# Delayed attention units, weight products in traced order, later norm steps and a split last norm in a decoder layer

## The chip, the cores and the metric

The kernel runs on one core of one Trainium2 chip. The metric is the device time of one execution in microseconds (us). The core's engines are named as in the profile: PE (TensorE, matrix products; PEld is its weight load), DVE (VectorE), ACT (ScalarE), POOL (GpSimd) and SP (SyncE, which here only issues DMAs). Each engine works through its own list of instructions in order; semaphores tie the lists together.

## The reference

One decoder layer on 256 tokens of width 2048, in fp32. `D_FF` is 5632.

```python
def swiglu(h, w_gate, w_up, w_down):
    return (jax.nn.silu(h @ w_gate) * (h @ w_up)) @ w_down
...
    x = x + 0.5 * swiglu(rms_norm(x, ffn1_norm), ...)
    x = gated_parallel_mixer(x, mix_norm, w_in, ...)
    x = memory_cross_attention(x, mem, cross_norm, ...)
    x = x + 0.5 * swiglu(rms_norm(x, ffn2_norm), ...)
    return rms_norm(x, final_norm)
```

The mixer multiplies the normed x by `w_in` and sends parts of the result two ways. One is attention within a window of 128 tokens, with 16 heads in 4 groups and a sink added to each softmax:

```python
    m = jnp.maximum(jnp.max(s, axis=-1, keepdims=True), sink)
    e = jnp.exp(s - m)
    p = e / (jnp.sum(e, axis=-1, keepdims=True) + jnp.exp(sink - m))
```

The other is a recurrent token mixing (RWKV-7) with a state of 64 by 64 for each of 16 heads. For it the keys are shifted between neighbouring tokens, normalised (`kk / max(sqrt(sum(kk*kk)), 1e-12)`, the "removal keys") and weighted with a decay and a rate. Both results are projected, gated with a sigmoid, added and multiplied by `w_out`.

## The kernel before

**Products.** Every fp32 weight is loaded by SP into `raw` and split into two parts: `hi`, a rounding cast on ACT (L396), and `lo`, the residue on DVE (L397). The activations are split the same way (`xhi`, `xlo`). A product is then three matmuls, written by `times` in lines L473, L474 and L475, which add up in an accumulator `acc` in PSUM. There are three buffers of `acc`, three of `mm` and two of `tr`. `multiply` does `KU` = 2 slices of the inner dimension for one half of the tokens, so it issues six matmuls (a "group of six"). `product` loops over the weight units of a column block and over the two halves of the tokens, and calls `bg.tick()` after each group of six.

**Background steps.** `bg` is an `Interleave`: named groups of Python generators. A tick lets the first generators of each group (two in "attn" and "chain", four in "stage", one in the others) run on to their next `yield`. `idle(n)` yields n times, `wait_for(name)` yields until a name has been reported. So the distance between two steps is counted in ticks, that is, in groups of six. This fixes the order in which the instructions are traced. A scheduler behind it may move instructions of an engine against that order, where tiles and buffers allow; `tc.issue_after(ins)` keeps what is written under it behind the instruction `ins`.

**Attention.** `attend(kv, qb)` handles one group of heads and one block of 128 queries: scores (L903), scale and bias (L909), maximum (L916 to L923), exponentials with their sums on ACT (L926, L928), normalisation on DVE (L936), transposes (L942) copied to `pt` on ACT (L945), and the product with v (L950), split into `yahi` (L957) and `yalo` (L958). Eight such generators are spawned in the order kv, qb; two run at a time.

**Columns.** `columns` multiplies by `w_in`, scales the result into `tok` (L847, ACT), transposes it (L661) into `p` (L975, ACT), forms the difference of neighbours `d` (L978, POOL) and the mix of both (L982, DVE). `decay_and_rate` loads its small weights `wa` with two DMAs on POOL's queue (L1009, L1010) and multiplies by them (L1023). `removal_keys(h)` does the normalisation: sums of squares on PE (L1081), root on ACT (L1082), maximum and reciprocals on DVE (L1084, L1086), the factors of `kk` (L1088 to L1099), products `kk` by `at` (L1118) and their mask (`lt`, L1124). The blocks `lt` go to DRAM (`ld`) and come back by four SP loads as `dl` (L1139) for a triangular substitution on DVE (L1146). Gates (`ga`) take a sigmoid on ACT (L1168) and a product on DVE (L1171). The chain of the token mixing (L1249 transposes, L1255 `mk`, L1286 to L1329 products) runs beside later columns, and `stage` (L376 to L388) forms sums of weights for the second feed-forward from tiles `su` and `sg`.

**Output projection and norms.** The product with `w_out` is added to x on DVE (L1480). Then `n3.block` transposes x (L661), scales it into `xhi` (L688) and `xlo` (L689) and takes squares (L697). In the last feed-forward `done2` adds up squares of a finished block of 512 columns (L1587, ACT) and multiplies the block by the final gain (L1589, POOL). After the last matmul come the sum (L769), its squares, the mean (L707, L708), the power on POOL (L710), the scaling (L1601 to L1605) and the store (L1608).

Of the kernel before, what the change touches and what calls it, by code (L numbers as in the profile page):

```python
# [136 lines left out]
def decoder_layer(ctx: ExitStack, tc: tile.TileContext, a: dict, out: bass.AP):  # L137
# [31 lines left out]
    def wait_for(name):  # L169
        while name not in bg.seen:  # L170
            yield

    def idle(n):
        for _ in range(n):
            yield


    ones = cpool.tile([P, P], F32, name="ones")
    pool.memset(ones[:], 1.0)
# [148 lines left out]
    raws, parts, summed = {}, {}, {}  # L328
    first_unused = {items[i][0][1] for i in staged}
    sums_d = dram.tile([len(staged), P, 4, 512], F32, name="sums")  # L330
    at = {"item": 0, "product": 0, "pool": None}

    def load(u, pieces=None):

# [135 lines left out]
    def times(o, x, w, first, last, **how):  # L470

        (xh, xl), (hi, lo) = x, w
        pe.matmul(o, xh, hi, start=first, stop=False, **how)  # L473
        pe.matmul(o, xh, lo, start=False, stop=False, **how)  # L474
        pe.matmul(o, xl, hi, start=False, stop=last, **how)  # L475

    def multiply(o, x, u, k, t, nk):
        s = slice(t * P, (t + 1) * P)
        for i in range(KU):
            times(  # L480
                o, [x.at(p, k + i)[:, s] for p in range(2)], [w[:, i, :] for w in u],
                k + i == 0, k + i == nk - 1,
            )

    def combinations(sp, x: Act, seven, name, ready=lambda: True, early=True, n=0):

# [227 lines left out]
    def feed_forward(sp, x, norm: Norm, wg, wu, wd, done, begin_last=lambda: None, last=False):  # L714
# [13 lines left out]
        for gi, (j0, nj) in enumerate(GROUPS):  # L728
            h = Act(
                [sp.tile([P, 16, T], F32R, tag="hhi", name="hhi")],  # L730
                [sp.tile([P, 16, T], F32R, tag="hlo", name="hlo")], 16,
            )
            ch = combinations(sp, h, SEVEN_DOWN[nj < 4], "d", early=False, n=12)

            def transposed(hb, c):
                for q in range(2):
                    split(h, c + 2 * q, 2, feat(hb, [2 * q * P, (2 * q + 1) * P]))
                    yield

            for j in range(j0, j0 + nj):  # L740
                if j > 0:
                    hb = gate_and_up(sp, norm.x, c, norm.r, wg)

                    c["next"].append(transposed(hb, 4 * (j - j0)))
                    continue
                pg = product(norm.x, wg)
                hb = sp.tile([P, 2, 512], F32, tag="hb", name="hb", bufs=2)
                for t in range(2):
                    act.activation(hb[:, t, :], pg[t][:], AF.Silu, scale=norm.r[t])
                pu = product(norm.x, wu)  # L750
                for t in range(2):
# [12 lines left out]
            for n in (0, 2):  # L764
                if last and end and n:
                    for m in (n, n + 1):
                        pd = product(h, wd, skew=m == 3)
                        for t in range(2):
                            dve.scalar_tensor_tensor(  # L769
                                col(t, m), pd[t][:], 0.5, col(t, m), ALU.mult, ALU.add  # L770
                            )
                        done(m)
                    continue
                down(sp, h, ch, wd, [[col(t, n + i) for i in range(2)] for t in range(2)])
                if end:
                    done(n)
                    done(n + 1)
# [11 lines left out]

    def aligned(sp):  # L790

        sp.tile([P, 16], F32, name="shift")


    with tc.tile_pool(name="f1", bufs=1, reuse_waits="tile") as sp:
# [32 lines left out]
    with tc.tile_pool(name="mx", bufs=1, reuse_waits="tile") as sp:  # L828
# [645 lines left out]
        for n in range(4):  # L1474
# [3 lines left out]
            po = product(mt, W["w_out"])  # L1478
            for t in range(2):
                dve.tensor_tensor(s[:, t, :], po[t][:], s[:, t, :], ALU.add)  # L1480
            bg.spawn("feat", n3.block(n, s))
            if n == 0:
                bg.spawn("mem", memory())

# [70 lines left out]


    with tc.tile_pool(name="f2", bufs=1, reuse_waits="tile") as sp:
        aligned(sp)
        at["pool"] = sp
        x = sp.tile([P, 2, D], F32, name="x")  # L1560
        fins = []
# [1 line left out]
        def fin(n):  # L1563

            return fins[n // 2][:, n % 2]

        def gain():
            for n in range(4):
# [3 lines left out]
                pool.dma_start(fin(n), a["final_norm"][cb].unsqueeze(0).broadcast_to([P, 512]))  # L1572
                yield

        def reload():
            for n in range(4):
                cb = slice(n * 512, (n + 1) * 512)
# [1 line left out]
                pool.dma_start(x[:, :, cb], blk(x3d, n))  # L1579

        bg.spawn("const", reload())
        ss = stat.tile([P, 2, 4], F32, tag="ss", name="ss")

        def done2(n):
            for t in range(2):
                xs = x[:, t, n * 512 : (n + 1) * 512]
                act.activation(junk_t[:], xs, AF.Square, accum_out=ss[:, t, n : n + 1])  # L1587
# [51 lines left out]
```

## Time and profile before

| what | value |
|---|---|
| median of three runs | 2249.39 us (2248.35 to 2249.53) |
| profiled execution, own time | 2248.79 us |
| its span, first to last instruction | 2247.1 us |
| mean granted clock of TensorE | 0.999 |
| PE / PEld busy | 2231.4 / 1833.6 us |
| DVE / ACT / POOL busy | 1820.5 / 1245.0 / 134.9 us |
| mean DMA throughput | 205 GB/s |

A row of the timeline reads: start in us from the span's start, duration in us, engine, line, operation, output and inputs by tile name, shapes, number of instructions, and in brackets the idle time of the engine just before and what ended it. Several like instructions that follow each other are one row (x4), and its duration runs over all of them. In the view of waits a row reads: engine, tile and line that waited, engine, tile and line waited for, total us, number of times, longest. A matmul's duration in a row holds its passage through the array, so matmuls of 0.39 us start about 0.227 us apart.

### The profile page before, as it was taken

To read this page: it belongs to the slowest core of one execution; us is meant where nothing else is said; L and a number is where in the kernel's file an instruction comes from. 1 tells how busy PE (TensorE), PEld (TensorE's weight loads), DVE (VectorE), ACT (ScalarE), POOL (GpSimd) and SP (SyncE) were. 2 spreads that over 40 slices of the span, in tenths; PEclk is the share of its full clock that TensorE was granted. 3 is DMA by queue.
4 is the path that set the end of the run, shared out by engine and by line. 5 is a ranking of instruction groups with operands and counts; after the bars stand their busy time and mean duration, and the time that the engine had idled before them with its cause. 6 is when DMAs were issued, how large, how long until landed. Compare 5 with 4: busy or idle time off the path is not lost.

```text
span 2247.1 us, 28239 instructions
## 1 busy us (share of the span) xinstructions
PE 2231.4 (99%) x10587; PEld 1833.6 (82%) x10587; DVE 1820.5 (81%) x2342; ACT 1245.0 (55%) x1621; POOL 134.9 (6%) x192
## 2 busy tenths in 40 slices
PE   9999999999999999999999999999999999999998
PEld 7888888888888877788888888888888888888886
DVE  7898988998989476977656666547999999999997
ACT  6555555555556567544444446456665466555654
POOL 1000000000001000201320040001000000000002
PEclk9999999999999999999999999999999999999999
DMA  7555555556556544676767576547565566556564
GB/s 264 187 201 197 201 198 202 200 188 212 195 193 201 169 135 150 198 231 207 224 214 263 187 258 227 190 167 272 197 237 204 195 231 218 201 205 221 197 229 146
DMA packets 229225, 461.35 MB, mean 205 GB/s; under 512 B 15227, under 2 KB 17504, under 8 KB 229088
## 3 DMA queue, kind: packets, MB, share of 16 engines
q1 hardware_dynamic: 220512, 433.62, 56.8%
q0 software_dynamic: 8112, 25.12, 3.5%
q8 instruction: 83, 1.36, 0.2%
q10 hardware_dynamic: 464, 0.79, 0.1%
q14 instruction: 54, 0.44, 0.1%
HBM read 435.91 MB, written 23.59 MB: 204 GB/s over the span
## 4 chain that ended last, share of the span: by engine, by line
PE 95%; DVE 2%; DMA 1%; issue 1%; ACT 1%; SPq 0%; POOL 0%; POOLq 0%; DVEq 0%; ACTq 0%
PE acc L473 19%; PE acc L474 19%; PE acc L475 19%; PE mm L475 8%; PE mm L474 8%; PE mm L473 8%; PE tr L661 2%; PE tr L474 2%; PE tr L473 2%; PE tr L475 2%; PE mm L1313 1%; DVE lo L397 1%; PE tr L1249 1%; DMA raw<-in_w_out_dram 0%; PE mm L903 0%
## 5 line engine op out<-in xcount | busy, mean ns | idle before, releaser
L396 ACT CAST hi<-raw 128x1024 fp32r<-128x1024 f32 (+1 forms) x770 | 756.5, 992 | 714.4 <-PE acc L475 514.8
L397 DVE TENSOR_TENSOR lo<-raw,hi 128x1024 fp32r<-128x1024 f32 (+1 forms) x770 | 886.1, 1153 | 315.5 <-ACT hi L396 314.0
L473 PE MATMUL acc<-hi,xhi 128*128 128x512 f32 (+1 forms) x1166 | 462.2, 397 | 2.1 <-ACT xhi L688 1.7
L474 PE MATMUL acc<-lo,xhi 128*128 128x512 f32 (+1 forms) x1166 | 452.7, 388 | 0.0
L475 PE MATMUL acc<-hi,xlo 128*128 128x512 f32 (+1 forms) x1166 | 452.5, 388 | 0.0
L473 PEld LDWEIGHTS acc<-hi,xhi 128*128 128x128 f32 x1166 | 219.4, 188 | 49.8 <-issue 4.0
L475 PEld LDWEIGHTS acc<-hi,xlo 128*128 128x128 f32 x1166 | 218.8, 188 | 46.0 <-DVE xlo L689 1.0
L474 PEld LDWEIGHTS acc<-lo,xhi 128*128 128x128 f32 x1166 | 219.2, 188 | 43.8 <-issue 1.7
L404 ACT CAST thi<-raw 128x1024 fp32r<-128x1024 f32 x192 | 199.9, 1052 | 62.9 <-DVE raw L427 42.4
L405 DVE TENSOR_TENSOR tlo<-raw,thi 128x1024 fp32r<-128x1024 f32 x192 | 232.2, 1219 | 1.1 <-ACT thi L404 0.4
L474 PE MATMUL acc<-lo,hhi 128*128 128x512 f32 x372 | 145.5, 391 | 0.8 <-DVE lo L397 0.8
L475 PE MATMUL acc<-hi,hlo 128*128 128x512 f32 x372 | 145.5, 391 | 0.0
L473 PE MATMUL mm<-hi,xhi 128*128 128x512 f32 x370 | 145.4, 393 | 0.0
L473 PE MATMUL acc<-hi,hhi 128*128 128x512 f32 x372 | 144.9, 390 | 0.0
L475 PE MATMUL mm<-hi,xlo 128*128 128x512 f32 x370 | 144.3, 390 | 0.0
L474 PE MATMUL mm<-lo,xhi 128*128 128x512 f32 x370 | 144.2, 390 | 0.0
L474 PEld LDWEIGHTS acc<-lo,hhi 128*128 128x128 f32 x372 | 69.9, 188 | 15.4 <-DVE lo L397 1.2
L473 PEld LDWEIGHTS acc<-hi,hhi 128*128 128x128 f32 x372 | 69.9, 188 | 14.3
L475 PEld LDWEIGHTS mm<-hi,xlo 128*128 128x128 f32 x370 | 69.4, 188 | 14.6
L475 PEld LDWEIGHTS acc<-hi,hlo 128*128 128x128 f32 x372 | 69.9, 188 | 14.0
L474 PEld LDWEIGHTS mm<-lo,xhi 128*128 128x128 f32 x370 | 69.5, 188 | 14.2
L473 PEld LDWEIGHTS mm<-hi,xhi 128*128 128x128 f32 x370 | 69.5, 188 | 14.0
(396 smaller groups left out, 3595.7 us busy)
## 6 DMA issues: line engine op xcount, KB each, us to landing
raw<-in_ffn_w_down_dram SPq DMA_DIRECT2D x88, 1024.0 KB, 5.1
raw<-in_ffn_w_gate_dram SPq DMA_DIRECT2D x84, 1024.0 KB, 5.1
raw<-in_ffn_w_up_dram SPq DMA_DIRECT2D x78, 1024.0 KB, 6.2
raw<-in_w_in_dram SPq DMA_DIRECT2D x136, 512.0 KB, 3.5
raw<-in_w_out_dram SPq DMA_DIRECT2D x32, 512.0 KB, 4.4
raw<-sums SPq DMA_DIRECT2D x20, 512.0 KB, 6.3
raw<-in_w_proj_attn_dram SPq DMA_DIRECT2D x16, 512.0 KB, 4.4
raw<-in_w_proj_rwkv_dram SPq DMA_DIRECT2D x16, 512.0 KB, 4.8
```

Of the source, the lines that this page charges most:

```text
L396: at["hi"] = act.copy(hi[:, s], raw[:, s])
L397: at["lo"] = dve.tensor_tensor(lo[:, s], raw[:, s], f32(hi[:, s]), ALU.subtract)
L404: act.copy(hi[:], v[:])
L405: dve.tensor_tensor(lo[:], v[:], f32(hi[:]), ALU.subtract)
L473: pe.matmul(o, xh, hi, start=first, stop=False, **how)
L474: pe.matmul(o, xh, lo, start=False, stop=False, **how)
L475: pe.matmul(o, xl, hi, start=False, stop=last, **how)
L661: pe.transpose(b[:, o : o + P], tok[:, t, col : col + P], ident[:])
L1249: pe.matmul(b[e][:, o : o + P], x1[r, j, cs_], x2[r, j, cs_], start=True, stop=True)
L1313: pe.matmul(vb[:, (o + k) * P : (o + k + 1) * P][:, r], lhs(k, e), rhs[:, k, r], start=first and k + e == 0, stop=True, **ek,)
```

## The change

1. `times` returns its last matmul. While the weights come from the shared pool (`at["pool"] is None`, that is, between the two feed-forwards), each three matmuls of `multiply` are issued behind the three before: the scheduler may no longer exchange weight products.
2. `attend(0, 1)`, the unit of the first heads' second query block, idles four ticks before it starts. The units after it in the queue run as places come free.
3. `n3.block`, the norm step on a finished block of the output projection, starts two ticks later (`later_by`).
4. In the last feed-forward, the multiplies by the final gain become a background generator `gained`, which idles three ticks, and `bg.drain()` runs what is left of them behind the feed-forward. For the last block of 512 columns the sum is made in two pieces of 256 columns; the squares of the first piece are taken on ACT, those of the second on DVE. The sums of squares lie in the tile "shift" and have a fifth column.

```diff
+    def later_by(n, steps):
+        yield from idle(n)
+        yield from steps
...
-    at = {"item": 0, "product": 0, "pool": None}
+    at = {"item": 0, "product": 0, "pool": None, "w": None}
...
-        pe.matmul(o, xl, hi, start=False, stop=last, **how)
+        return pe.matmul(o, xl, hi, start=False, stop=last, **how)
...
         for i in range(KU):
-            times(
-                o, [x.at(p, k + i)[:, s] for p in range(2)], [w[:, i, :] for w in u],
-                k + i == 0, k + i == nk - 1,
-            )
+            with tc.issue_after(at["w"].ins) if at["w"] else nullcontext():
+                w = times(
+                    o, [x.at(p, k + i)[:, s] for p in range(2)], [w[:, i, :] for w in u],
+                    k + i == 0, k + i == nk - 1,
+                )
+            at["w"] = w if at["pool"] is None else None
...
+                    whole = [(t, slice(0, 512)) for t in range(2)]
+                    parts_ = [(t, slice(c, c + 256)) for t in range(2) for c in (0, 256)]
+                    pieces = {2: whole, 3: parts_}
                     for m in (n, n + 1):
                         pd = product(h, wd, skew=m == 3)
-                        for t in range(2):
+                        for t, cs in pieces[m]:
                             dve.scalar_tensor_tensor(
-                                col(t, m), pd[t][:], 0.5, col(t, m), ALU.mult, ALU.add
+                                col(t, m)[:, cs], pd[t][:, cs], 0.5, col(t, m)[:, cs],
+                                ALU.mult, ALU.add,
                             )
-                        done(m)
+                            done(m, t, cs)
...
             yield from wait_for("kv")
+            if kv == 0 and qb:
+                yield from idle(4)
...
-            bg.spawn("feat", n3.block(n, s))
+            bg.spawn("feat", later_by(2, n3.block(n, s)))
...
+        def gained(t, n):
+            yield from idle(3)
+            xs = x[:, t, n * 512 : (n + 1) * 512]
+            pool.tensor_tensor(xs, xs, fin(n), ALU.mult)
...
-        def done2(n):
-            for t in range(2):
-                xs = x[:, t, n * 512 : (n + 1) * 512]
-                act.activation(junk_t[:], xs, AF.Square, accum_out=ss[:, t, n : n + 1])
+        ss = room[:, :10].rearrange("p (t n) -> p t n", t=2)
+
+        def done2(n, t=None, cs=slice(0, 512)):
+            for t in range(2) if t is None else (t,):
+                xs = x[:, t, n * 512 : (n + 1) * 512][:, cs]
+                if cs.start:
+                    dve.scalar_tensor_tensor(
+                        junk_t[:, cs], xs, 1.0, xs, ALU.mult, ALU.mult, accum_out=ss[:, t, 4:5]
+                    )
+                else:
+                    act.activation(
+                        junk_t[:, cs], xs, AF.Square, accum_out=ss[:, t, n : n + 1]
+                    )
                 if n < 3:
-                    pool.tensor_tensor(xs, xs, fin(n), ALU.mult)
+                    bg.spawn("ew", gained(t, n))
...
+        bg.drain()
```

More of the change, by code (lines that the diff above doesn't have):

```diff
@@ L790, in aligned @@
     def aligned(sp):
-        sp.tile([P, 16], F32, name="shift")
+        return sp.tile([P, 16], F32, name="shift")
     with tc.tile_pool(name="f1", bufs=1, reuse_waits="tile") as sp:
@@ L1557, in decoder_layer @@
     with tc.tile_pool(name="f2", bufs=1, reuse_waits="tile") as sp:
-        aligned(sp)
+        room = aligned(sp)
         at["pool"] = sp
@@ L1581, in decoder_layer @@
         bg.spawn("const", reload())
-        ss = stat.tile([P, 2, 4], F32, tag="ss", name="ss")
-        def done2(n):
-            for t in range(2):
-                xs = x[:, t, n * 512 : (n + 1) * 512]
-                act.activation(junk_t[:], xs, AF.Square, accum_out=ss[:, t, n : n + 1])
+        ss = room[:, :10].rearrange("p (t n) -> p t n", t=2)
[10 more added lines that the diff above has]
+                    )
                 if n < 3:
-                    pool.tensor_tensor(xs, xs, fin(n), ALU.mult)
+                    bg.spawn("ew", gained(t, n))
         feed_forward(
```

## The prediction

> **What bounds the kernel now.** I read the page's busy times first, then its chain, then TensorE's waits, and only then single stretches of the timeline. Busy times and chain:
>
> ```profile
> PE 2231.4 (99%) x10587; PEld 1833.6 (82%) x10587; DVE 1820.5 (81%) x2342; ACT 1245.0 (55%) x1621; POOL 134.9 (6%) x192
> ...
> PE 95%; DVE 2%; DMA 1%; issue 1%; ACT 1%; SPq 0%; POOL 0%; POOLq 0%; DVEq 0%; ACTq 0%
> ```
>
> TensorE is busy 99% of the span and carries 95% of the chain. A change that leaves all matmuls in place can move the end in two ways only: by what it costs to pass from one kind of matmul to another, and by waits of TensorE. The view of waits tells how much there is to win (line waited for: us in total, times, longest):
>
> ```profile
> PE tr L661 <- ACT tok L847: 0.8, 1, 0.8
> PE acc L474 <- DVE lo L397: 0.8, 1, 0.8
> PE tr L661 <- DVE x L1480: 0.8, 2, 0.5
> ...
> PE tr L1249 <- DVE mk L1255: 0.3, 1, 0.3
> PE mm L1118 <- DVE lt L1124: 0.3, 1, 0.3
> PE tr L661 <- DVE yalo L958: 0.3, 1, 0.3
> ...
> PE tr L1286 <- DVE mk L1255: 0.2, 1, 0.2
> PE mm L903 <- DVE s L909: 0.2, 1, 0.2
> ```
>
> All of these but the second lie in the changed stretches: 2.9 us, 0.13% of the time. So a gain beyond 0.2% (4.5 us, about what a measurement of this kernel can tell from no change) can't come from waits alone. All sums below are made on the profiled execution, 2248.79 us (span 2247.1 us and 1.7 us around it); the median of the runs, 2249.39 us, is 0.03% above it.
>
> **The change part by part.** Both kernels issue 10038 matmuls of the same shapes. Set side by side, the two orders on TensorE differ in the attention and removal keys (786 to 983 us of the trace), the chain of the second token mixing (1092 to 1275), the output projection (1363 to 1444), and nowhere else by more than a few instructions.
>
> *Switches.* Weight products now keep the order in which they are traced, so the small products of attention and chain stand between whole groups of six. Counted in the orders, passes from small products to weight products rise from 423 to 447: 10 more in attention and keys, 18 more in the chain, 4 fewer at the output projection. One pass, by the first weight product behind a group of small ones and the next of its kind:
>
> ```profile
> 1137.50 0.49 PE L473 MATMUL acc<-hi,xhi 128*128 128x512 f32 x1
> ...
> 1138.30 0.40 PE L473 MATMUL acc<-hi,xhi 128*128 128x512 f32 x1
> ```
>
> 0.09 us each: 24 x 0.09 = 2.2 us at most by this row, and 0 if every new pass falls beside a wait. I take 1.5, nearer the row.
>
> *The delayed unit of attention.* Two units run at a time, one per query block of a key head. Four ticks more for query block 1 of kv 0 carry it past its partner, so that the units of all four heads are paired differently. The place that pays is the start of the next columns, where today these rows stand:
>
> ```profile
> 809.15 0.39 ACT L928 ACTIVATE s<-s,nm 128x128 f32<-128x128 f32 x1
> ...
> 813.31 0.59 ACT L945 COPY pt<-tr 128x512 f32<-128x512 f32 x1 [0.85 <-PE tr L942]
> ...
> 815.83 0.91 ACT L847 ACTIVATE tok<-acc,rs 128x288 f32<-128x288 f32 x2
> ...
> 816.39 0.33 PE L661 MATMUL tr<-ident,tok 128*128 128x128 f32 x1 [0.76 <-ACT tok L847]
> ```
>
> In the new order the transposes of the scores of kv 1 come directly in front of the transposes of tok. VectorE has a weight residue and four normalisations ahead of them; by hand TensorE stands 0.9 us there. The copy pt (0.59) then follows those transposes and tok (0.46 for its first half) follows the copy on ScalarE: with two hand-overs of 0.2 (an estimate), 1.45 us more. Now: 0.8 + 0.3 + 0.2 = 1.3 of waits, 2.4 with the smaller gaps counted from start to start. Bounds -1.3 (all waits gone) to +1.1 (2.35 against 1.3); I take 0, the two counted alike.
>
> *The weights wa of decay and rate.* POOL's queue is passed over too. Its two loads stand 25 us ahead of their use now; in the new order both stand behind the second d (L978) of the first removal keys.
>
> ```profile
> 826.03 0.54 POOL L1010 DMA_DIRECT2D wa<-in_rwkv_a_dram  x1
> ...
> 853.46 0.59 ACT L975 COPY p<-tr 128x512 f32<-128x512 f32 x1 [0.26 <-PE tr L661]
> ...
> 854.13 1.04 POOL L978 TENSOR_TENSOR d<-p 128x512 f32<-128x512 f32 x1 [1.19 <-ACT p L975]
> ...
> DMA to landing us min/median/max: 3.8/3.8/3.8
> ...
> DMA to landing us min/median/max: 6.3/6.3/6.3
> ```
>
> From the end of p's transposes: 0.3 to the copy, 0.67 to d, 1.04 for d, 0.6 for the first load, 6.3 to the landing of the second: 8.9 us. TensorE has about 34 weight products of 0.227 or small groups of that length before wa, 7.7 us: 1.2 us of wait, or 0 if it lands as fast as the other one did (3.8). I take 0.6.
>
> *Removal keys.* ScalarE's order now has a gate's sigmoid (L1168) between the two square roots (L1082) of each half, so the tables are swapped six times in this stretch instead of four.
>
> ```profile
> 896.67 0.60 ACT L1082 ACTIVATE sq<-tr 128x512 f32<-128x512 f32 x1 [1.16 <-PE tr L1081]
> ...
> 897.30 0.43 DVE L1084 TENSOR_SCALAR sq<-sq 128x512 f32<-128x512 f32 x1 [0.18 <-ACT sq L1082]
> 897.76 1.75 DVE L1086 RECIPROCAL sq<-sq 128x256 f32<-128x256 f32 x1
> ...
> 937.00 1.28 ACT L1168 ACT_TABLE_LOAD   x1
> 937.29 1.16 DVE L397 TENSOR_TENSOR lo<-raw,hi 128x1024 fp32r<-128x1024 f32 x1
> 938.29 1.27 ACT L1168 ACTIVATE ga<-acc,rs 128x512 f32<-128x512 f32 x2
> 938.37 1.22 DVE L1088 TENSOR_TENSOR kk<-kk,sq 128x1024 f32<-128x1024 f32 x1
> ...
> 912.88 0.49 PE L1118 MATMUL mm<-kk,at 64*128 64x128 f32 x2
> ```
>
> For the second half: half a sigmoid 0.64, a load 1.28, the root 0.60, then VectorE's queue up to the last factor of kk: 0.43, two reciprocals of 1.75, eight passes of 1.22 (four of them weight residues), one half-pass of 0.64 and 0.2: 14.5. Together 17.0 us, against 66 weight products, 15.5 us with 0.4 of a pass: late by 1.1. Behind it lt, which frees one of three mm buffers, is late by 0.6 (0.64 a piece, two pieces). The first half by the same walk: 0.9. Sum 2.6, against 1.24 from start to start today (0.77 at 912.88 and 0.47 at 948.05): +1.4. Bounds 0 (products wait no longer than now) and 2.6 (none of today's wait goes).
>
> Here the Trainium skill speaks against the change more strongly than these rows: "ScalarE: Activation LUTs", section "What ACT_TABLE_LOAD costs", gives 1.28 us for the load and as much as 1.38 us more for a drain with every switch. The trace agrees on the load (1.28) and shows no drain: the sigmoid starts 0.01 us behind the load. By the page each half would be 1.4 us later.
>
> *The chain.* Its tok has a cast in front on ScalarE; the difference sums of staged weights (su, sg) get a second pair of loads only when the first pair's stores have gone out.
>
> ```profile
> 1112.00 1.28 DVE L1255 TENSOR_TENSOR mk<-tr,mask 128x512 f32<-128x512 f32 x2
> ...
> 1113.74 0.69 DVE L380 TENSOR_TENSOR sg<-su,sg 128x512 f32<-128x512 f32 x1 [0.46 <-DMA sg<-in_ffn_w_gate_dram]
> ```
>
> Now this DMA holds VectorE 0.46 us, and mk 0.5 us of TensorE. New: 0.55 on tok, 0.25 on its follower, 0.4 to 1.9 on mk behind L380. Against about 1.5 from start to start today: -0.5 to +1.2; I take +0.3.
>
> *Norm steps two ticks later.*
>
> ```profile
> 1364.71 0.39 PE L475 MATMUL acc<-hi,mtlo 128*128 128x512 f32 x1
> 1364.85 1.28 DVE L1480 TENSOR_TENSOR x<-acc,x 128x512 f32<-128x512 f32 x2
> 1365.58 0.14 PEld L661 LDWEIGHTS tr<-ident,x 128*128 128x128 f32 x1 [0.91 <-DVE x L1480]
> ...
> 1366.18 0.31 PEld L661 LDWEIGHTS tr<-ident,x 128*128 128x128 f32 x3 [0.46 <-DVE x L1480]
> ```
>
> The transposes of x wait for both sums and lose 0.64 + 0.5 us. Later by two ticks they wait for nothing. But six more weight products take their place, and they write the third accumulator, which the first of the same two sums sets free: TensorE reaches it at 1364.94 and the sum ends at about 1365.5, 0.55 us. Gain 0.6 (bounds 0 and 1.1).
>
> *Last norm.* POOL's multiplies by the gain still wait for the same squares on ScalarE, and POOL has nothing else to do: three ticks in the trace leave their start where it was, and with it the slow residues behind the 0.8 us wait on lo. The end, in two halves:
>
> ```profile
> 2238.46 0.69 DVE L769 SCALAR_TENSOR_TENSOR x<-acc,x 128x512 f32<-128x512 f32 x1 [0.30 <-PE acc L475]
> ...
> 2239.94 0.16 DVE L707 TENSOR_REDUCE ms<-ss 128x1 f32<-128x4 f32 x1 [0.79 <-ACT junk L1587]
> ...
> 1367.27 0.48 DVE L689 SCALAR_TENSOR_TENSOR xlo<-tr,gains,xhi 128x256 fp32r<-128x256 f32 x1
> ```
>
> A 256-wide piece costs 0.48. Three on VectorE, one behind the other, end at 2238.46 + 1.44 = 2239.90 against 2239.94: 0. Bounds -0.3 (they overlap by 0.1 each) and +0.2 (the accumulated sum is read late).
>
> Sum: 1.5 + 0 + 0.6 + 1.4 + 0.3 - 0.6 + 0 = +3.2, 2248.8 + 3.2 = 2252.0 us: slower than the median by 0.12%, within what can be told.
>
> **The rivals.**
> - The waits go and no new ones come: transposes in clean groups give VectorE and ScalarE more time. For it speaks that each wait today is a single event. Against it, the copy and tok stand in one queue behind the new transposes. Price: 2.9 us of waits, passes hidden: 2245.9 us.
> - The triangular blocks (dl) become the wait: slower than can be told. Two weight loads now stand ahead of their four loads on SP's queue, and the loads that follow wait for them.
>
> ```profile
> 959.07 4.19 SPq L1139 DMA_DIRECT2D dl<-ld  x4
> ...
> 963.36 0.51 SPq L355 DMA_DIRECT2D raw<-in_w_in_dram  x1
> ```
>
>   They hold SP for 4.3 us; by hand dl goes out 5 us later and the weight behind it is ready 1.5 us ahead of use. From 1.5 us of further delay on it decides; as long again as they hold SP gives 2252.0 + 4.3 = 2256.3 us. Against it: the slack is positive.
> - Table swaps cost their drain (the page's rule): 1.4 us more at each half of the keys, 2252.0 + 2.8 = 2254.8 us. Against it stands the 0.01 us above.
> - Nothing moves: the orders differ but new passes and waits balance, 2248.8 us.
>
> **How the numbers follow.** Forecast 0.50 (2249.5 to 2255); waits gone 0.24; dl 0.14; table swaps 0.05; nothing 0.07. Faster by over 0.2% is under 2244.9, reached only by the first rival's lower tail: 0.06. Slower by over 0.2% is above 2253.9: dl and swaps, and three tenths of the forecast's own case: 0.34. Within: 0.60. The range runs from 2245.2, the first rival with 0.7 less, to 2256.8, dl with 0.5 more.
>
> **What would show it.** Waits of TensorE on tok near 812 us of some 1.4 instead of 0.8, and one on s ahead of it; a wait on wa under 1.2; six table loads on L1082 and L1168's new lines instead of four; the wait on x replaced by one of an accumulator near 1365; POOL's multiplies starting 0.3 us behind their squares as now. The prediction is wrong if TensorE's waits in 786 to 983 come to less than 1.6 us, or if a DMA stands among them with more than 2.

## The result: 14 us slower, and the profile after

| | before | after |
|---|---|---|
| median | 2248.87 us (2248.10 to 2249.53, 4 runs) | 2263.03 us (2259.40 to 2265.37, 4 runs) |
| span of the profiled execution | 2247.1 us | 2261.3 us |

The ratio is 1.0064, with a 95% interval of 1.0052 to 1.0076. The forecast was 2252.0 us, in a range up to 2256.8: the direction was right, the size and the range were not.

The page of the changed kernel, busy times and chain:

```profile
PE 2237.5 (99%) x10587; PEld 1835.3 (81%) x10587; DVE 1827.4 (81%) x2348; ACT 1246.1 (55%) x1623; POOL 132.9 (6%) x192
...
PE 90%; DVE 4%; DMA 2%; ACT 1%; issue 1%; SPq 0%; POOL 0%; POOLq 0%; DVEq 0%; ACTq 0%
```

TensorE's share of the chain falls from 95% to 90%, VectorE's and the DMAs' rise. TensorE's waits in the changed kernel (line waited for: us in total, times, longest):

```profile
PE tr L668 <- ACT tok L859: 2.0, 3, 1.3
PE mm L1132 <- DVE lt L1138: 1.9, 1, 1.9
PE tr L668 <- DVE mk L1269: 1.9, 1, 1.9
...
PE acc L478 <- DVE lo L401: 1.5, 2, 0.8
PE acc L477 <- DVE ga L1185: 1.4, 2, 0.8
PE acc L477 <- DVE x L1494: 1.1, 1, 1.1
...
PE tr L1300 <- DVE mk L1269: 1.0, 1, 1.0
PE tr L1263 <- ACT vtok L1219: 0.7, 1, 0.7
PE tr L956 <- DVE s L950: 0.6, 2, 0.3
```

(L668, L859, L1132, L1138, L1185, L1269 and L1494 are L661, L847, L1118, L1124, L1171, L1255 and L1480 of before.) All rows of this view add up to 14.8 us, against 7.2 before. So waits explain about half of the 14 us. The other half lies between the waits. Since both kernels issue the same matmuls, the start of a matmul with the same number can be compared in the two traces (numbered by the 10038 matmuls that the kernel issues; the profile's x10587 has 549 of them as two records each):

| matmul number | starts before | starts after | later by | what lies in between |
|---|---|---|---|---|
| 3520 | 786.5 | 786.3 | -0.1 | |
| 4000 | 890.9 | 891.4 | +0.6 | attention, wa |
| 4400 | 982.9 | 991.6 | +8.8 | removal keys |
| 4890 | 1092.1 | 1100.1 | +8.0 | gates |
| 5715 | 1274.7 | 1288.1 | +13.4 | chain |
| 6500 | 1443.7 | 1457.6 | +13.9 | output projection |
| last | 2238.0 | 2252.4 | +14.4 | second feed-forward |

Two places carry nearly all of it: the removal keys (+8.2) and the chain (+5.4). And there is something that no wait shows. Four stretches of the changed kernel by the view of windows (stretch, its length, busy us and instructions of PE, PEld, DVE, ACT, POOL, then PEclk, the granted clock, and the DMAs):

```profile
812.00:814.00 2.00, 1.84 (x7) 1.51 (x8) 0.44 (x4) 1.75 (x8) 0.00 (x0) 0.65 0.29 112
814.00:816.00 2.00, 2.00 (x8) 0.96 (x6) 1.05 (x2) 1.33 (x4) 1.04 (x1) 0.50 0.02 4
...
960.00:965.00 5.00, 3.31 (x13) 2.78 (x14) 5.00 (x6) 0.00 (x0) 3.74 (x3) 0.78 0.76 252
965.00:970.00 5.00, 5.00 (x21) 4.02 (x20) 1.75 (x2) 1.79 (x2) 1.65 (x3) 0.88 0.83 274
```

The granted clock falls to one half for a while behind two of the waits. TensorE is busy there, and each weight product takes 0.43 us from start to start instead of 0.23. Eight slow matmuls at 963 us and five at 814 us are 8 x 0.2 + 5 x 0.22 = 2.7 us.

The three new waits in the timeline of the changed kernel (start, duration, engine, line, what, and the idle time before with its releaser). First attention:

```profile
809.65 0.87 DVE L950 TENSOR_SCALAR s<-s,den 128x128 f32<-128x128 f32 x4
...
811.14 0.56 ACT L959 COPY pt<-tr 128x512 f32<-128x512 f32 x1
...
811.61 0.90 ACT L859 ACTIVATE tok<-acc,rs 128x288 f32<-128x288 f32 x2
...
812.16 0.33 PE L668 MATMUL tr<-ident,tok 128*128 128x128 f32 x1 [1.25 <-ACT tok L859]
```

This is the place that the prediction walked: normalisation, transposes, copy pt, tok, each behind the other. Then the second half of the removal keys:

```profile
957.59 2.37 POOL L1122 TENSOR_TENSOR kt<-kt,aa 128x1024 f32<-128x1024 f32 x1 [29.48 <-DVE aa L1118]
957.93 3.11 DVE L401 TENSOR_TENSOR lo<-raw,hi 128x1024 fp32r<-128x1024 f32 x1
...
960.70 2.55 POOL L1123 TENSOR_TENSOR aa<-kt,cs 128x1024 f32<-128x1024 f32 x1
960.96 1.27 DVE L1138 TENSOR_TENSOR lt<-mm,mask_l 128x512 f32<-128x512 f32 x2
961.69 1.16 PE L1132 MATMUL mm<-kk,at 64*128 64x128 f32 x8 [1.89 <-DVE lt L1138]
...
963.37 0.63 PE L479 MATMUL acc<-hi,xlo 128*128 128x512 f32 x1
963.79 0.63 PE L477 MATMUL acc<-hi,xhi 128*128 128x512 f32 x1
```

VectorE has a weight residue queued in front of lt, and beside a multiply on POOL this one residue takes 3.11 us instead of 1.22: 1.89 us more, as much as the wait. Before, a residue beside this multiply stands behind lt (949.24 against 947.80), and TensorE waits 0.3 us. The clock falls right behind the new wait. Last the chain:

```profile
1120.30 0.69 DVE L384 TENSOR_TENSOR sg<-su,sg 128x512 f32<-128x512 f32 x1 [1.31 <-DMA sg<-in_ffn_w_gate_dram]
...
1121.02 0.69 DVE L385 TENSOR_TENSOR su<-su 128x512 f32<-128x512 f32 x1
...
1123.49 1.53 DVE L389 TENSOR_TENSOR sg<-sg,su 128x512 f32<-128x512 f32 x1
...
1124.94 1.21 DVE L866 TENSOR_TENSOR kl<-kt,kh 128x1024 fp32r<-128x1024 f32 x1
...
1126.08 1.21 DVE L401 TENSOR_TENSOR lo<-raw,hi 128x1024 fp32r<-128x1024 f32 x1
...
1127.21 1.28 DVE L1269 TENSOR_TENSOR mk<-tr,mask 128x512 f32<-128x512 f32 x2
...
1127.95 0.66 PE L668 MATMUL tr<-ident,tok 128*128 128x128 f32 x4 [1.89 <-DVE mk L1269]
```

Before, mk at 1112.00 came ahead of the staged sums (L384 to L389 are L380 to L385 there). Now the four sums, a residue, kl and another residue stand in front of it. This wait of 1.89 us, as long as the one at 961, left the clock alone: the first weight product behind it takes 0.47 us, not 0.63. Why is seen with the inserted waits below.

### The profile page after: what moved, and what is told of

The parts are those of the page before. It is cut to its first block, busy times and chain, and to the rows that moved or that the text cites. A ratio compares the mean times of both kernels' runs of the same rounds, so it can differ in the third digit from the quotient of the medians.

```text
span 2261.3 us, 28255 instructions
## 1 busy us (share of the span) xinstructions
PE 2237.5 (99%) x10587; PEld 1835.3 (81%) x10587; DVE 1827.4 (81%) x2348; ACT 1246.1 (55%) x1623; POOL 132.9 (6%) x192
## 4 chain that ended last, share of the span: by engine, by line
PE 90%; DVE 4%; DMA 2%; ACT 1%; issue 1%; SPq 0%; POOL 0%; POOLq 0%; DVEq 0%; ACTq 0%
PE acc L477 18%; PE acc L478 18%; PE acc L479 18%; PE mm L478 7%; PE mm L479 7%; PE mm L477 7%; PE tr L668 2%; PE tr L478 2%; PE tr L477 2%; PE tr L479 2%; DVE lo L401 2%; PE mm L1327 1%; DMA raw<-in_ffn_w_up_dram 1%; PE tr L1263 1%; ACT hi L400 1%
## 5 line engine op out<-in xcount | busy, mean ns | idle before, releaser
L478 PEld LDWEIGHTS mm<-lo,xhi 128*128 128x128 f32 x370 | 69.5, 188 | 14.2
```

## The experiments

The kernel before ran beside each group of kernels, and its median moved between 2247.7 and 2249.3 us from one group to the next. So kernels of different groups are compared by their ratios to before; 0.001 is 2.2 us.

**Which part of the change is it?** Four kernels, each with a part of it. The delay alone is these two lines in `attend` of the kernel before:

```diff
             yield from wait_for("kv")
+            if kv == 0 and qb:
+                yield from idle(4)
```

> The kernel before with the four idle ticks of the unit (kv 0, query block 1) alone. Theory A (the delay moves attention, keys and chain and makes the new waits): 9 to 14 us slower than before, that is 2258 to 2263 us, with a wait of mm on lt near 960 us and of tr on mk near 1126 us of 1.5 us or more each. Theory B (the traced order of the weight products makes them, the delay only its own part at 811 us): 1 to 3 us slower, 2250 to 2252 us.

Measured: 2255.70 us against 2248.75, ratio 1.0033 (1.0021 to 1.0044). Between the two theories: 7 us, half of the loss. Waits on lt (1.0) and on wa (0.9) are there, the wait on mk is only 0.2. By matmul numbers the keys lose 5.2 us here and the chain 2.2.

The traced order alone is the edit of `times` and `multiply`:

```diff
+            with tc.issue_after(at["w"].ins) if at["w"] else nullcontext():
+                w = times(...)
+            at["w"] = w if at["pool"] is None else None
```

> The kernel before with the weight products held in traced order alone. Theory A: within 1.5 us of before, 2248 to 2251 us. Theory B: 9 to 13 us slower, 2258 to 2262 us, with the waits on lt and mk.

Measured: 2253.00 us, 1.0021 (1.0011 to 1.0030). Again between the two. Here all of the loss lies at 810 to 820 us (+3.6 at matmul 3760, +4.0 at the end). The timeline of this kernel:

```profile
813.03 1.23 PE L945 MATMUL tr<-ident,s 128*128 128x128 f32 x8 [1.21 <-DVE s L939]
...
815.14 0.91 ACT L850 ACTIVATE tok<-acc,rs 128x288 f32<-128x288 f32 x2
815.71 0.47 PE L664 MATMUL tr<-ident,tok 128*128 128x128 f32 x1 [1.46 <-ACT tok L850]
815.84 0.77 PE L473 MATMUL acc<-hi,xhi 128*128 128x512 f32 x1
```

Without delay the traced order takes away the weight products that stood between scores, transposes and tok. TensorE waits 1.21 us for the normalised scores and 1.46 for tok, and then runs slow too (0.77 for a product).

The changed kernel without the delay (the two lines above taken out again):

> The changed kernel without the four idle ticks. Theory A: 2248 to 2251 us, what is left being the wait on x near 1364 us (up to 0.5 us more than before). Theory B: 2259 to 2262 us.

Measured: 2252.96 us, 1.0018 (1.0009 to 1.0028), the same as the order alone, at the same place. The rest of the change alone (`later_by` and the last norm, in the kernel before):

> The kernel before with the later norm steps and the last norm in halves alone. Both theories: between 0.6 us faster and 0.6 us slower than before, 2248.3 to 2249.5 us. The trace of the changed kernel shows 0.5 us lost at the output projection and 0.1 at the end, so I expect the slower half.

Measured: 2248.35 us, 0.9998 (0.9989 to 1.0008): nothing, as expected of the part. Delay and order alone cost 7.0 and 4.3, together with the norms 14.2: some 3 us more than the sum. Neither theory holds as it was put; both edits make waits, and with both in place the long waits in the chain are new.

**What makes the keys late?** Both roots of a half are issued one behind the other, so that the sigmoid of a gate can't come between them:

```diff
-            for i in (0, 2):
+            sqs = [sq[:, i : i + 2, :].rearrange("p c t -> p (c t)") for i in (0, 2)]
+            for sq2 in sqs:
                 b = tr()
-                sq2 = sq[:, i : i + 2, :].rearrange("p c t -> p (c t)")
                 pe.matmul(b[:], bdones[:], sq2, start=True, stop=True)
                 act.activation(sq2, b[:], AF.Sqrt)
-                yield
+            yield
+            for i, sq2 in zip((0, 2), sqs):
+                if i:
+                    yield
                 dve.tensor_scalar(sq2, sq2, 1e-12, None, ALU.max)
```

> The changed kernel with both roots of a half of the removal keys issued one behind the other, so that no gate's sigmoid stands between them and the tables are swapped four times instead of six. Theory A (the second root behind a sigmoid and two swaps makes the keys late): the waits on ga, lo and lt between 913 and 963 us, 4.6 us together, fall below 2, and no slow clock follows at 963: 3 to 5 us faster than the changed kernel, 2258 to 2260 us. Theory B (VectorE's weight residues in front of the factors of kk make it late, the swaps are hidden): less than 1 us faster, 2262 to 2263 us.

Measured: 2256.19 us, ratio to before 1.0035 (1.0022 to 1.0047), 6.5 us faster than the changed kernel and beyond what both theories had. The waits on lt and ga leave the list of the longest, and the clock stays up behind the keys. Matmul 4400 starts 2.5 us later than before instead of 8.8. Of these 6.2 us, 1.4 are won ahead of the keys, in the attention, which the edit leaves alone: there the clock did not fall in this run, which is luck (why is seen with the inserted waits below). Between matmuls 4000 and 4400 this kernel loses 3.2 us and the changed one 8.2. So 4.9 us of the keys' loss come from the late second root and what follows from it, the clock included; the run doesn't say what makes the other 3.2. With the roots together the residue in front of lt falls differently: it takes 2.53 us beside POOL's multiply and the wait on lt is 0.5 (with the delay alone 3.10 and 1.0). That it was the table load itself is not shown: see the six ticks below. The chain isn't mended: it loses 6.4 us here.

**What makes mk late?** The staged sums begin 64 weight units later, behind the chain:

```diff
-STAGE_AT = [266 + 2 * n for n in range(10)]
+STAGE_AT = [330 + 2 * n for n in range(10)]
```

> The changed kernel with the staged sums of weights (su, sg) begun 64 weight units later, behind the chain. Theory A (VectorE stands in front of mk and vtok's followers for these loads and sums): the waits on mk of 1.9 and 1.0 us and on vtok of 0.7 fall below 1 us together, 3 to 4 us faster than the changed kernel, 2259 to 2260 us. Theory B (the chain's new order puts residues and kl in front of mk, staging or not): less than 1 us faster, 2262 to 2263 us.

Measured: 2282.09 us, 1.0149 (1.0134 to 1.0165): a loss of 19 us on the changed kernel. In the chain theory A held: the waits on mk fall from 2.9 to 0.5 us, that on vtok goes, and matmul 5100 starts 7.0 us later than before instead of 13.8 (1.6 of these 6.8 us were gained ahead of the chain). But the loads now run beside those for w_out, which hold SP and VectorE there: 11.6 us of waits on hi and 3.7 on lo between 1380 and 1500 us.

The other way, 24 units earlier (242 in place of 266):

> The changed kernel with the staged sums begun 24 weight units earlier, ahead of the chain instead of beside it; beside it or behind it are then none of the first pairs. Theory A (loads and sums of su and sg stand in front of mk on VectorE): the waits on mk of 1.9 and 1.0 us go, as they did with later staging, and nothing takes their place: 4 to 6 us faster than the changed kernel, 2257 to 2259 us. Theory B (what was won with later staging was won by the shifted chain order, not by VectorE): less than 2 us faster, 2261 us or more.

Measured: 2272.36 us, 1.0106 (1.0090 to 1.0121). The waits on mk go again, and 12 us are lost among the gates in front of the chain (waits on lo rise to 6.4 us in the whole run, those on tok to 4.8). The same with the roots together:

> The changed kernel with the roots together and the staged sums earlier. If the two causes are separate, their gains add: 6.8 us and 4 to 6 us, that is 2250 to 2253 us, the rest being attention (tok) and the clock behind it. If they are one (a late start carried along), 2255 us or more.

Measured: 2267.00 us, 1.0085 (1.0071 to 1.0098). The roots' gain is there a second time (5.4 us against staging_earlier), the gates' loss too. And earlier staging in the kernel without delay and order:

> The kernel before with the later norm steps, the last norm in halves and the earlier staging, without delay and without traced order: a try for a kernel that beats both. The waits on mk near 1112 and 1115 us (0.5 us of waits, about 1 us from start to start) go: 2247.0 to 2248.2 us, 0.3 to 1.5 us faster than before. If the earlier sums make waits of their own, 2249 us or more.

Measured: 2261.47 us, 1.0064 (1.0052 to 1.0077): 13 us lost at the gates. All of these missed: that work which is moved away costs nothing at its new place was wrong three times.

Then only the sums are moved, by two ticks:

```diff
-        yield from idle(4)
+        yield from idle(6)
         u0, u1, g0, g1 = (e[:, c] for e in t for c in range(KU))
```

> The changed kernel with the staged sums (L384 to L389) two ticks later behind their loads, the loads as they were. Theory A (VectorE waits in its queue 1.3 us for sg in front of kl and mk): the wait on mk of 1.9 us falls below 0.7 and that of 1.0 with it, 2.5 to 4 us faster than the changed kernel, 2259 to 2261 us. Theory B (kl and two residues in front of mk make it late by themselves): the wait stays above 1.3 us, 2262 to 2264 us.

Measured: 2260.58 us, 1.0052 (1.0038 to 1.0066), 2.7 us faster than the changed kernel, with intervals that overlap, and not for the reason given:

```profile
1125.92 1.27 DVE L1269 TENSOR_TENSOR mk<-tr,mask 128x512 f32<-128x512 f32 x2
...
1126.65 0.66 PE L668 MATMUL tr<-ident,tok 128*128 128x128 f32 x4 [2.07 <-DVE mk L1269]
```

VectorE no longer waits for sg (the sums start right behind a residue at 1120.14), yet mk is as late as before. The load wasn't the cause of this wait. With staging_later, where kl and a residue still stand ahead of mk and the sums don't, the wait is 0.5; so the cause is the four sums in the queue (3.5 us). The later waits, on the second mk and on vtok, are gone here, but the clock falls behind this wait (half from 1128.1 to 1134.9 us), and the chain loses 6.5 us, more than the changed kernel's 5.4. The 2.7 us are won elsewhere: 1.5 in the attention, where the clock happened to stay up, 1.2 at the output projection and 1.1 behind it, less what the chain loses.

**Does the order matter behind the attention?** The traced order is held only once the attention is done:

```diff
-            at["w"] = w if at["pool"] is None else None
+            at["w"] = w if at["pool"] is None and "attn" in bg.seen else None
```

> The changed kernel with the traced order held only from the end of the attention on. Theory A (in the attention the small products want free weight products between them as cover): the waits on s and tok at 809 to 813 us and the slow clock behind them go, 2 to 3 us faster than the changed kernel, 2260 to 2261 us. Theory B (the delay alone makes the wait on tok): 2262 to 2264 us.

Measured: 2262.17 us, 1.0062 (1.0047 to 1.0077): no difference, the time of theory B. At matmul 3680 the kernel is 3.0 us ahead of the changed one, as theory A says. Then TensorE arrives at wa ahead of its load and waits 0.9 us; at the keys 1.3 us of the lead are left, behind the chain 0.7. A wait that is removed early is waited out later.

**Does a wait bring the clock down?** In the kernel before, eight waits are put into the products with w_proj_rwkv and w_out, by this helper:

```diff
+    def gap(n):
+        b = tr()
+        with tc.issue_after(at["last"].ins):
+            pe.transpose(b[:, :P], ident[:], ident[:])
+        act.copy(held, b[:, :P])
+        for _ in range(n - 1):
+            act.copy(held, held)
+        at["hold"] = pe.transpose(b[:, P : 2 * P], held, ident[:])
```

> The kernel before with eight waits put into the products with w_proj_rwkv and w_out (1290 to 1410 us): TensorE transposes a block, ScalarE copies it 3, 6, 9, 12, 5, 8, 11 and 7 times over, TensorE transposes the copy, and all weight products stay behind it. At 0.27 us a copy the waits are about 1.1, 1.9, 2.7, 3.5, 1.7, 2.5, 3.3 and 2.2 us. The result is not changed by them. Theory A (a wait of somewhat under 2 us can already bring the granted clock down to half for about 3.3 us): each wait above some point between 1.5 and 2 us is followed by matmuls 0.43 us apart instead of 0.227; 20 us of waits and 5 to 8 times 1.6 us of slow clock, 2277 to 2283 us. Theory B (the slow stretches at 814 and 963 us belong to something else than the waits): 2268 to 2271 us and the clock stays at 1.00.

Measured: 2294.67 us, 1.0206 (1.0186 to 1.0226), outside both ranges. The copies were slower than assumed and the waits longer, 1.85 to 5.95 us; the sixth of them was broken up by transposes of another step, which leaves seven. The two shortest of them and the third in the timeline:

```profile
1305.33 0.33 PE L497 MATMUL tr<-ident,junk 128*128 128x128 f32 x1 [1.85 <-ACT junk L496]
...
1373.91 0.33 PE L497 MATMUL tr<-ident,junk 128*128 128x128 f32 x1 [2.56 <-ACT junk L496]
...
1320.48 0.33 PE L497 MATMUL tr<-ident,junk 128*128 128x128 f32 x1 [2.89 <-ACT junk L496]
```

Waits of 1.85 and 2.56 us leave the clock at 1.00; from 2.89 us on each of the other five is followed by half the clock, with weight products 0.43 us apart for some 2 to 4.7 us. So a wait does bring the clock down (theory B falls). But its length alone doesn't decide, as theory A had it: 2.56 us passed here, and in the changed kernel 1.89 us did it at 961 us and did not at 1128, and 1.25 us did it at 812, where a shorter wait (0.25 on s at 810) stands close by.

The times at which the granted clock changes show what else decides. In the changed kernel it falls at 812.61 and 962.80 us and rises again 3.41 us behind each fall; from the first fall to the second it is 150.19 us, 44 times 3.413. In each of the 20 kept traces all changes of the clock lie on one such grid of 3.413 us, and where the grid lies against the kernel's start differs from trace to trace. Here is the view of windows laid on the grid, three stretches and the one behind the last of them for the changed kernel, then twice a stretch and the one behind it for the inserted waits:

```profile
809.20:812.61 3.41, 1.90 (x10) 1.10 (x9) 3.21 (x13) 1.98 (x7) 0.00 (x0) 1.00 0.49 153
...
959.39:962.80 3.41, 1.52 (x11) 0.99 (x9) 3.41 (x4) 0.00 (x0) 3.39 (x3) 1.00 0.47 154
...
1126.64:1130.05 3.41, 2.10 (x19) 1.86 (x20) 2.64 (x5) 0.59 (x1) 0.69 (x1) 1.00 0.94 274
1130.05:1133.46 3.41, 2.37 (x15) 1.69 (x14) 2.92 (x6) 1.04 (x1) 1.66 (x4) 1.00 1.04 398
```

```profile
1317.42:1320.83 3.41, 0.52 (x4) 0.35 (x3) 1.82 (x2) 2.85 (x8) 0.00 (x0) 1.00 0.89 335
1320.83:1324.24 3.41, 3.41 (x9) 2.65 (x9) 0.69 (x1) 0.00 (x0) 0.16 (x1) 0.50 0.39 135
...
1372.03:1375.45 3.42, 1.54 (x7) 1.30 (x8) 1.71 (x2) 1.70 (x6) 0.00 (x0) 1.00 1.03 399
1375.45:1378.86 3.41, 3.41 (x16) 2.82 (x15) 0.73 (x1) 1.05 (x1) 0.00 (x0) 1.00 1.03 386
```

A stretch's length less PE's busy time is what TensorE stood still in it. In the changed kernel it is 1.51 and 1.89 us in the first two, and the clock is halved behind both. The grid cuts the wait at 1128: 1.31 us lie in one stretch, and the clock stays. Of the inserted waits, the one of 2.89 us lies in one stretch; the one of 2.56 us is cut, with 1.88 in the larger part. Over all kept traces, stretches at full clock with 1.9 us or more of standstill are always followed by half the clock, and between 1.4 and 1.9 both occur. Below 1.4 us the clock fell only twice, behind 1.00 us with the delay alone and 0.77 with the roots together; small products fill much of both stretches, and what counts besides the standstill stays open. So the same waits cost the clock or not by where they fall on the grid. That is also why the attention's waits halve the clock in the changed kernel and not with the roots together: there the largest standstill in one of these stretches is 1.26 us.

The Trainium skill, "TensorE: Matmul & The Clock Gate", Part 1, has the clock fall after an idle window of about 3.4 us and lets this window run freely. The grid agrees with the window's length and its running freely; that waits well under a window can be enough does not agree with it.

**Is it the delay, or this delay?** The changed kernel with six and with eight ticks:

```diff
             if kv == 0 and qb:
-                yield from idle(4)
+                yield from idle(6)
```

> The changed kernel with six idle ticks instead of four. Theory A (any delay that pairs the units anew costs about the same): 2259 to 2266 us, with waits on lt and mk of over 1.5 us again. Theory B (each number of ticks lays the steps of attention, keys and chain differently against each other, and four fell badly): off by more than 3 us from the changed kernel, to either side; the place of the waits changes.

> The changed kernel with eight idle ticks instead of four. Theory A (the cost goes by how the steps happen to fall against each other): anywhere from 2246 to 2266 us, and not between four and six by any rule; a time above 2255 us goes with waits of over 1.3 us of TensorE. Theory B (more delay is better, once four is passed): 2246 to 2249 us.

Measured: 2248.49 us with six (1.0004, 0.9995 to 1.0013) and 2262.88 us with eight (1.0063, 1.0049 to 1.0076). Four, six and eight ticks give +14, 0 and +14 us. These three show no rule in the number. With eight the waits stand elsewhere (2.6 and 1.4 us on mk, 1.1 on tok). With six, matmul 3920 is 4.3 us ahead of the kernel before, and the keys give 3.6 us of it back. The table loads, by groups between 880 and 1000 us, before and with six ticks:

```profile
L1082 ACT ACT_TABLE_LOAD x2 | 2.6, 1283 | 0.0
L1168 ACT ACT_TABLE_LOAD x2 | 2.6, 1283 | 0.0
```

```profile
L1096 ACT ACT_TABLE_LOAD x3 | 3.8, 1283 | 0.1
L1182 ACT ACT_TABLE_LOAD x3 | 3.8, 1283 | 0.1
```

Six loads here too, with a wait on lt of only 0.3 us (the residue stands behind lt again), and the keys lose 3.6 us instead of 8.2. With six ticks alone, the last kernel of the next part, six loads go with 1.4 us. So it isn't the swaps alone that make the loss. What they and the late root still cost with six ticks is seen next.

**A kernel that beats both.** Six ticks, once without the traced order, once with the roots together, once with both, and once the six ticks alone in the kernel before; the edits are those shown.

> The changed kernel with six ticks and without the traced order of the weight products. If the traced order costs its own 4 us wherever it is (as it did alone), this is 2244 to 2246 us; if its cost was the waits at 811 to 814 us, which six ticks have removed, 2247.5 to 2250 us.

> The changed kernel with six ticks and the roots together: a try for a kernel that beats both. The table loads fall from six to four. If the loads cost only where products wait for the keys: the waits on ga at 909 and 948 us (1.5 us) shrink by half, 2247 to 2248.5 us. If the loads cost their own length (2.6 us) on the path: 2245.5 to 2246.5 us.

> The changed kernel with six ticks, without the traced order and with the roots together. If the waits on ga, which the roots together shortened by about 1.4 us beside the traced order, cost the same here: 2244 to 2245 us. If the free order has already hidden them: 2245 to 2246.5 us.

> The kernel before with six idle ticks of the unit (kv 0, query block 1) alone. If the alignment of that one unit is the whole matter: 2245 to 2247 us, where four ticks gave 2255.7. If the later norms carry part of the gain: 2247 to 2249 us.

| kernel | median | ratio to before | 95% interval |
|---|---|---|---|
| six ticks, norms, free order | 2245.63 us | 0.9985 | 0.9976 to 0.9994 |
| six ticks, norms, traced order, roots together | 2247.11 us | 0.9989 | 0.9980 to 0.9998 |
| six ticks, norms, free order, roots together | 2246.35 us | 0.9992 | 0.9983 to 1.0001 |
| six ticks alone | 2246.11 us | 0.9990 | 0.9981 to 0.9999 |

The whole change but the traced order, with six ticks, beats both kernels by a little (0.15% against before), and the six ticks alone do nearly as well: 0.9990 where four gave 1.0033. So the gain is that unit's, and the later norms add nothing that can be told. The traced order still costs 3 to 4 us with six ticks (1.0004 against 0.9985; 2.9 us between the traces). The time is the first theory's, but the place is new: 1.8 us in the keys, 1.1 in the chain and 0.3 in the attention, where alone it cost all of its 4 us. TensorE's waits between 786 and 1300 us of the table's first kernel:

```profile
PE tr L1260 <- DVE mk L1266: 0.5, 1, 0.5
PE tr L1212 <- DVE mk L1266: 0.5, 1, 0.5
PE tr L665 <- ACT tok L856: 0.2, 1, 0.2
```

That is 1.2 us; the same stretch of the changed kernel has 6.3 + 4.0 = 10.3. The roots together win 1.4 us by the medians and 3.4 by the ratios beside the traced order (1.0004 to 0.9989, with intervals that overlap; 1.7 us between matmuls 4000 and 4400), and nothing beside the free one.

## Why the prediction was wrong

*Removal keys: this step failed.* The mechanism was named in part (second root behind a sigmoid and a swap, then VectorE's queue, then lt). The term was mis-sized: +1.4 predicted, with an upper bound of 2.6, and +8.2 measured between matmuls 4000 and 4400, with the passes there, which the prediction had put under switches. The last link, lt, was taken as two pieces of 0.64 us with nothing in front; it came behind a weight residue that took 3.11 us beside POOL's multiply instead of 1.22, and the wait was 1.89. The clock then added 1.6. The working has a slip as well: 17.0 against 15.5 us is 1.5 late and not 1.1, which makes the term +1.8. The prediction's rival fell that the drain of 1.4 us a switch would decide, which the Trainium skill gives ("ScalarE: Activation LUTs", "What ACT_TABLE_LOAD costs"): the roots together do mend most of the keys, but no drain is seen (in the changed kernel, as before, the activation starts 0.01 us behind the load), and with six ticks alone six swaps go with a loss of 1.4 us in the keys.

*The chain: this step failed.* +0.3 predicted, with +1.2 as the upper end (the lower end, -0.5, is -0.3 by its own terms), +5.4 measured. The prediction followed the loads of su and sg to mk; what stood in front of mk were the four sums themselves, with kl and two residues: 1.89, then 1.0 on the second mk and 0.7 on vtok. The bound was the fault: it took the longest single delay, and not that three waits in a row can each be new.

*The granted clock: missing altogether.* The prediction let the change act through passes and waits alone; slower matmuls are a third way. The profile before shows 0.999 for the whole run and no wait over 1.1 us, so nothing there prices it. About 2.7 us of the profiled execution are slow matmuls, and it shows in the scatter of the runs: 2259.4 us at a mean clock of 0.998, 2265.4 at 0.996.

*Attention and wa.* +0.6 predicted, about +0.7 measured; that the sums agree is luck. The wait on tok was walked rightly (1.45 predicted, 1.25 measured; the one ahead of it 0.9 against 0.25 here). Slow matmuls took 1.1 us that were not foreseen. The wait on wa did not come, because TensorE arrived late; where it came earlier (the delay alone, or the order held only behind the attention), it was 0.9 us (bound 1.2).

*Norm steps later.* -0.6 predicted, +0.5 measured in the profiled execution. The wait moved to the accumulator, as predicted, but was 1.15 us and not 0.55, behind a residue that started only at 1377.77:

```profile
1377.77 1.23 DVE L401 TENSOR_TENSOR lo<-raw,hi 128x1024 fp32r<-128x1024 f32 x1 [2.44 <-ACT hi L400]
...
1378.91 1.28 DVE L1494 TENSOR_TENSOR x<-acc,x 128x512 f32<-128x512 f32 x2
...
1379.65 0.50 PE L477 MATMUL acc<-hi,mthi 128*128 128x512 f32 x1 [1.15 <-DVE x L1494]
```

Other kernels with the same edit change by -0.7 to +0.9 us between matmuls 5715 and 6500. Within the error of a whole run it is nothing (the norms alone: 0.9998).

*Switches.* +1.5 predicted; no run isolates it. The counts 423 and 447 hold the passes both ways: from small products to weight products TensorE passes 212 times in the trace before and 224 times in the one after. So the upper end is 12 x 0.09 = 1.1 us, and 1.5 lay above it.

*Last norm.* 0 predicted. POOL's multiplies start 0.26 us behind their squares as before. From the last sum's start to the reduction it is 1.33 us now and was 1.48: right.

*The range.* It was built on the thought that one rival at a time comes true. Here keys, chain and clock came together. The clock fell because of two of the new waits. The chain's loss doesn't follow that of the keys: with the roots together they lose 3.2 us instead of 8.2, and it still loses 6.4. The test set for being wrong did not catch this: TensorE's waits between 786 and 990 us come to 6.3 us, not under 1.6, and no DMA stands among them. The signs came true for the most part (1.25 us on tok at 812, six table loads, the wait on an accumulator for that on x, POOL's 0.26 us): the places were right, and their prices were not.

## What to carry to other kernels

Where steps are placed by counting ticks, the number of ticks is not a size that costs more or less; four, six and eight gave +14, 0 and +14 us, and the right answer is to try the neighbours before explaining one of them. A walk through the new order must ask at each queue what stands ahead of the needed instruction, and a bound must let several waits in a row be new. Two waits of TensorE that look alike can differ by 1.6 us, because one of them is followed by half the clock; since this goes by the grid, a gain of that size can be luck.

## What the runs showed of the hardware

A wait of TensorE can halve its granted clock afterwards, for one or two stretches of 3.41 us: 5 to 11 weight products 0.43 us apart instead of 0.23. All changes of the clock in a trace lie on one grid of 3.413 us; what counts is how long TensorE stands still within one stretch of it. 1.9 us or more of it always halved the clock in the kept traces, less than 1.4 did so twice. Of seven inserted waits, those of 1.85 and 2.56 us did nothing and the five longer ones did it; in the changed kernel one of 1.25 us (with 0.25 close ahead) and one of 1.89 us did it, and another one of 1.89 did not. A weight residue on VectorE takes at most 1.23 us with no TENSOR_TENSOR of POOL beside it, in the traces before and after, and up to 3.11 beside one. A table load on ScalarE is 1.28 us, and the next activation starts at once.
